# A hybrid SSD decoder block on one core: the order of SSD products and late conditioning on TensorE

## Chip, core and metric

The kernel runs on one core of a Trainium2 chip. The metric is the device time of one execution in microseconds (us); the kernel before takes 1359.24 us, the median of three runs (1358.83 to 1359.36).

## What is computed

One layer of a decoder with 2048 channels. A prompt of 256 tokens and eight samples of four tokens are processed together, so that each activation is a matrix of 2048 channels by 288 columns. In the reference, cut to what matters here:

```python
mod = silu(c) @ w_ada + b_ada                    # six parts: sh1, sc1, g1, sh2, sc2, g2
h = rmsnorm(x, norm1) * (1 + sc1) + sh1
u_pool, z, xbc, dt_raw = split(h @ w_in)
pool_out = pool_mixer(u_pool)                    # trailing means, a small product per group
y = ssd(xs * dt, dt * A, Bm, Cm, h0)             # 24 heads of 64 in 4 groups, chunks of 128
#   y_diag = (C B^T * exp(cs_l - cs_s), masked) @ xdt ; y_off = C @ h_start * exp(cs)
y = rmsnorm((y + d_skip * xs) * silu(z), ssd_norm)
x = x + g1 * (concat(pool_out, y) @ w_out)
h2 = rmsnorm(x, norm2) * (1 + sc2) + sh2
x = x + g2 * (silu(conv(h2 @ w_gate)) * (h2 @ w_val)) @ w_down
```

All is in fp32.

## The kernel before

**Weights.** A weight tile of up to 128x1024 is loaded by SyncE's queue (`load`, L259 to L263), rounded by ScalarE to a high part whi (a cast, L281), and VectorE subtracts it from the raw tile to get the low part wlo (L283). The activations have such parts too. A block of 128x128 weights then takes three products of 288 columns (`mm3`, L293 to L297): whi with the high activations, whi with the low ones, wlo with the high ones. They are called weight products below. In the stage of the change eight raw tiles and two whi and two wlo tiles are there; a new load goes out when a raw tile is free again.

**Order.** A scheduler places the instructions of every engine when the program is built, from the order in which the code emits them, their dependencies and priorities; each engine then works through its own list in order. Instructions in `tc.high_priority()` go as early as they can; `tc.keep_in_program_order` fixes an instruction behind the ones emitted before it on its engine. The emission order is set by generators that the main loops advance: `pull(generator, rate)` adds the rate to a credit and advances the generator once for each whole credit.

**Stages.** To about 186 us: the first two conditioning parts and the first blocks of the input projection. Then dt, the last block of the xbc columns and, pulled in between, the four SSD groups; then the remaining u and z columns (uz, the loop around L1030) with SSD groups still going; at about 380 us the output projection (mm_out); from 507 us the MLP (up, gate, val, down) to the end.

**An SSD group** (`ssd_group`, L710) transposes its inputs (xt, bt), forms cb = C B^T with the causal mask, the chunk states s1 and s2, and the samples' part yo: 8 products that use a quarter of the array's columns each (L771, 16 records in the trace). Then for t = 0, 1, 2, two heads at a time:
- `decays(t)` (L782): a product cse broadcasts the cumulative sums of a head; ScalarE forms relu(cs_l - cs_s) into e for three column ranges (L794) and ec by exp (L795), then exp of all of e (L796); VectorE multiplies e by cb (L797) and ec by C (L798). e and ec have two buffers each.
- `outputs(t)` (L801): ten products into one PSUM tile y, two heads side by side, 64 rows each: yo with a selection matrix (L807), xdt of the samples with e (L810), xdt of chunk 0 (L813), xdt of chunk 1 (L816), and s1 with ec (L817). VectorE adds the skip term (L819), multiplies by the gate (L823), ScalarE squares (L825) and GpSimd sums (L829).

After the groups the sum of squares goes over partitions on TensorE (ysum, L235), the reciprocal root comes back as a broadcast (pbrstdy, L248), VectorE scales the gated y (zy, L898), and ScalarE and VectorE split it into mixh (L1059) and mixl (L1060), the operands of mm_out.

**Later conditioning.** Parts 2 to 5 of mod are formed by `ada_part_units` (L397). One k step takes two raw tiles of 512 KB, each for two products of 512 columns, with sc_c (silu of the nine conditions) as a stationary operand of 32 columns at one of four column positions (`ada_mm`, L321, product L324). `AY = 2` k steps make a visit: four loads and eight products (16 records, named adap). Eight visits, a copy to SBUF (asb), four transposes (adat) and VectorE's additions (L412) finish a part. The generator `adas` (parts 2, 3, 4) is pulled in the last xbc block at RA1/AY = 0.25 for each unit, in the uz loop at RA2/AY = 0.2 for each step of two k, at TA/AY = 2 ahead of mm_out (L1038) and in mm_out's loop (L1121); part 5 has its own generator (L1126). The scheduler may put other work between a visit's products.

Of the kernel before, what the change touches and what calls it, by code (L numbers as in the profile page):

```python
# [24 lines left out]
N = NP + NS  # L25
# [25 lines left out]
GB = 4  # L51
AY = 2

RA1, RA2, RB1, RB2, RB3 = 0.5, 0.4, 1.0, 1.0, 1.0
TA, ADA_OUT = 4, 4
TK = 4
GA = (2, 3)
# [104 lines left out]
def kernel(ctx: ExitStack, tc, ins, outs):  # L162
    nc = tc.nc
# [26 lines left out]
    seli = vec[:, K_SEL:K_SEL + 32]  # L190
# [9 lines left out]
    sc_c = kp.tile([P, KT, 32], F32, name="sc_c")  # L200
# [58 lines left out]
    def load(key):  # L259
        off, cols = S.items[key]  # L260
        t = wp[0].tile([P, RAWC], F32, tag="raw", name="raw_" + "_".join(map(str, key)))
        nc.sync.dma_start(t[:, :cols], wflat[off:off + P * cols].rearrange("(p n) -> p n", p=P))
        return t  # L263
# [54 lines left out]
        return ps  # L318


    def ada_mm(ps, raw, k, c0, nb, js):  # L321
        for j in js:
            c = c0 + (j - js[0]) * nb
            nc.tensor.matmul(ps[32 * j:32 * j + 32, :nb], sc_c[:, k, :], raw[:, c:c + nb],  # L324
                             start=(k == 0), stop=(k == KT - 1), tile_position=(0, 32 * j))

    def ada_sb(ps, nb, name, r=P):
        asb = kp.tile([P, 512], F32, tag="asb", name="asb_" + name)
        nc.scalar.copy(asb[0:r, :nb], ps[0:r, :nb])
        return asb  # L330

    def ada_tr(asb, nb, name, r=P):
        pt = aux("adat_" + name)
        for i in range(nb // P):
            nc.tensor.transpose(pt[:, i * r:(i + 1) * r], asb[0:r, i * P:(i + 1) * P], ident[0:r, 0:r])
        return pt

    def ada_scale(which, part, norm, k0, gk):
        nc.vector.scalar_tensor_tensor(
            out=amul[:, which, k0:k0 + gk, :], in0=ada[:, part, k0:k0 + gk, :], scalar=1.0,  # L340
            in1=norm[:, k0:k0 + gk].unsqueeze(2).to_broadcast([P, gk, NC9]),
            op0=ALU.add, op1=ALU.mult)

    def ada_group_units(gi):
# [49 lines left out]
            nc.vector.tensor_tensor(o, src, b.unsqueeze(3).to_broadcast([P, 2, nj // 2, NC9]), ALU.add)  # L394
        ada_scale(0, 1, early[:, V_N1:V_N1 + KT], k0, gk)

    def ada_part_units(part, ay=1):  # L397
        ps = pa.tile([P, 512], F32, tag="ada", name=f"adap{part}")
        for k in range(KT):
            raws = [load(("adap", part, k, h)) for h in range(2)]  # L400
            for h in range(2):
                ada_mm(ps, raws[h], k, 0, 512, range(2 * h, 2 * h + 2))
            if k % ay == ay - 1:
                yield
        asb = ada_sb(ps, 512, f"p{part}")
        yield
        pt = ada_tr(asb, 512, f"p{part}")
        for i in range(4):
            o = ada[:, part].rearrange("p (j i) c -> p j i c", j=4)[:, :, i, :]
            b = bada[:, part].rearrange("p (j i) -> p j i", j=4)[:, :, i]  # L410
            src = pt[:, i * P:(i + 1) * P].rearrange("p (j c) -> p j c", j=4)[:, :, 0:NC9]
            nc.vector.tensor_tensor(o, src, b.unsqueeze(2).to_broadcast([P, 4, NC9]), ALU.add)  # L412
        if part == 4:
            ada_scale(1, 4, vec[:, V_N2:V_N2 + KT], 0, KT)
        yield
# [65 lines left out]
    for q in range(4):  # L481
        t = mx.tile([P, 4, N], F32, tag="blk", name=f"xa{q}", bufs=4)
# [12 lines left out]
    sx = [None]  # L495
# [205 lines left out]
    def h0b(g, b):  # L701
        return h0t[g, b // 3][:, b % 3, :]
# [4 lines left out]
    def heads(ap):  # L707
        return ap.rearrange("p (h q) -> p h q", h=HG)

    def ssd_group(g):  # L710
        cf = cfs[g]
        cff = cf.rearrange("p m n -> p (m n)")
# [8 lines left out]
        xdt = kp.tile([P, 3, G6], F32, tag="hmod", name=f"xdt{g}", bufs=2)  # L721
# [27 lines left out]
        s1 = sx[0].tile([P, G6], F32, tag="s1", name=f"s1_{g}")  # L749
# [18 lines left out]
        for i in range(2):  # L768
            for j in range(4):
                b = 4 * i + j  # L770
                nc.tensor.matmul(py[32 * j:32 * j + 32, :G6], cm[:, 32 * b:32 * b + 32],  # L771
                                 h0b(g, b), start=(i == 0), stop=(i == 1),
                                 tile_position=(0, 32 * j))
        yo = sx[0].tile([P, G6], F32, tag="yo", name=f"yo{g}")
        nc.vector.tensor_tensor(yo.rearrange("p (h q) -> p h q", h=HG),
                                py[:, :G6].rearrange("p (h q) -> p h q", h=HG),
# [4 lines left out]

        def decays(t):  # L782

            e = sx[0].tile([P, 2, N], F32, tag="e", name=f"e{g}_{t}", bufs=2)
            ec = sx[0].tile([P, 2, P], F32, tag="ec", name=f"ec{g}_{t}", bufs=2)
            for i in range(2):
                hh = HG * g + 2 * t + i
                pe = aux(f"cse{hh}")
                nc.tensor.matmul(pe[:, :N], selr[:, hh:hh + 1].to_broadcast([P, P]), csr, start=True, stop=True)


                for c in range(3):
                    n = slice(c * P, min(c * P + P, N))
                    nc.scalar.activation(e[:, i, n], pe[:, n], AF.Relu, bias=cs[:, c, hh:hh + 1], scale=-1.0)  # L794
                nc.scalar.activation(ec[:, i, :], pe[:, P:NP], AF.Exp)  # L795
            nc.scalar.activation(e, e, AF.Exp, scale=-1.0)  # L796
            nc.vector.tensor_tensor(e, e, cb.unsqueeze(1).to_broadcast([P, 2, N]), ALU.mult)  # L797
            nc.vector.tensor_tensor(ec, ec, cf[:, 4, P:NP].unsqueeze(1).to_broadcast([P, 2, P]), ALU.mult)  # L798
            return e, ec

        def outputs(t, e, ec):  # L801
            assert (g, t) in zdone
            pq = aux(f"y{g}_{t}")
            rows = [slice(0, 64), slice(64, P)]
            for i, r in enumerate(rows):
                f = slice(64 * (2 * t + i), 64 * (2 * t + i) + 64)
                nc.tensor.matmul(pq[r, NP:N], yo[:, f], seli, start=True, stop=False)  # L807
            for i, r in enumerate(rows):
                f = slice(64 * (2 * t + i), 64 * (2 * t + i) + 64)
                nc.tensor.matmul(pq[r, NP:N], xdt[:, 2, f], e[:, i, NP:N], start=False, stop=True)  # L810
            for i, r in enumerate(rows):
                f = slice(64 * (2 * t + i), 64 * (2 * t + i) + 64)
                nc.tensor.matmul(pq[r, 0:P], xdt[:, 0, f], e[:, i, 0:P], start=True, stop=True)  # L813
            for i, r in enumerate(rows):
                f = slice(64 * (2 * t + i), 64 * (2 * t + i) + 64)
                nc.tensor.matmul(pq[r, P:NP], xdt[:, 1, f], e[:, i, P:NP], start=True, stop=False)  # L816
                nc.tensor.matmul(pq[r, P:NP], s1[:, f], ec[:, i, :], start=False, stop=True)  # L817
# [5 lines left out]
            nc.vector.tensor_tensor(zt, zt, yt, ALU.mult)  # L823
            sq = kp.tile([P, N], F32, tag="xsq", name=f"ysq{g}_{t}", bufs=2)
            nc.scalar.activation(sq, zt, AF.Square)  # L825
# [81 lines left out]
    adas = chain(*(ada_part_units(p, AY) for p in (2, 3, 4)))  # L907
    with in_order(*(e.engine for e in (nc.tensor, nc.scalar, nc.vector))):
# [3 lines left out]
        for q in range(4):  # L912
# [11 lines left out]
        first = [load(("xbc", 0, ci)) for ci in range(2)]  # L924
# [59 lines left out]
    def pull(gn, rate):  # L984

        credit[id(gn)] = credit.get(id(gn), 0.0) + rate
        while credit[id(gn)] >= 1:
            credit[id(gn)] -= 1
            next(gn, None)

    nloads[0] = len(first) + KT // 4
    for bi in range(len(BLOCKS)):
        last = bi + 1 == len(BLOCKS)
        top_up()
        if last:
# [5 lines left out]
            ps = pm.tile([P, 512], F32, tag="mm", name="mm_dt")  # L1001
# [23 lines left out]
    for m in list(range(4 + 3 * ZEARLY, 16)) + ULATE:  # L1025
        for _ in uz_units(m):
            n += 1
            for gn in late.values():
                pull(gn, 0.5)
            pull(adas, RA2 / AY)  # L1030
            pull(back, RB2 if n <= zlast else RB3)
            if n == zlast:
                drain(back)
                back = chain(ssd3, y_norm())
        if m < 4:
            late[m] = pool_units(m)
            next(late[m])
# [17 lines left out]
    for g in range(4):  # L1055
        for t in range(3):
            k = 4 + 3 * g + t
# [203 lines left out]
    rstdf, _ = rstd_of(psf, D, "rstdf", False)  # L1261
# [149 lines left out]
```

## Time and profile before

| quantity | before |
|---|---|
| median of three runs | 1359.24 us |
| the profiled execution's own time | 1359.61 us |
| its span in the trace | 1357.8 us |
| TensorE (PE) busy | 1342.5 us, 99% |
| VectorE (DVE) busy | 810.1 us, 60% |
| ScalarE (ACT) busy | 578.6 us, 43% |
| GpSimd (POOL) busy | 221.0 us, 16% |
| mean granted TensorE clock | 0.997 |
| DMA, mean over the span | 238 GB/s |

The page gives the busy time of each engine, its share in 40 slices of the span, and the chain of waits that ended last. In a timeline a row is: start, duration, engine, line, operation, output<-inputs, shape, number of records, and in brackets the idle time before it with the releaser. PE's records overlap, so that the time a product costs is the distance from its start to the next one's.

### The profile page before, as it was taken

What the parts mean: (1) busy time and instruction counts of PE and PEld (TensorE: products, weight loads), DVE (VectorE), ACT (ScalarE), POOL (GpSimd) and SP (SyncE); (2) the same over time, 40 slices, a digit from 0 to 9 for tenths busy, and PEclk for the clock granted to TensorE, in tenths of its full rate; (3) what the DMA queues carried; (4) which work ended last, traced back from release to release, by engine and by line L of the source; (5) the groups of instructions that cost most, each with busy time, mean ns of one, the idle gap of its engine ahead of it and who ended that gap; (6) DMA issues with size and microseconds to landing.
All of it is one profiled execution on the core that took longest, in us unless ns stands there. A gap on an engine that the chain in (4) does not pass through costs nothing.

```text
span 1357.8 us, 26226 instructions
## 1 busy us (share of the span) xinstructions
PE 1342.5 (99%) x10557; PEld 1247.4 (92%) x10557; DVE 810.1 (60%) x1349; ACT 578.6 (43%) x908; POOL 221.0 (16%) x428
## 2 busy tenths in 40 slices
PE   9999999999999999999999999999999999999997
PEld 7889988776779889999999999999999999999996
DVE  5775568778564448645565455656654556566543
ACT  5243234587643335534443334443433344434442
POOL 0000002122221213111221001212220011222221
PEclk9999999999999999999999999999999999999998
DMA  9999668877888877777555455555554555555531
GB/s 378 405 408 355 252 216 323 335 263 288 326 302 334 310 265 257 248 293 265 184 182 184 167 176 185 197 193 182 189 178 167 183 191 185 192 200 194 180 117 71
DMA packets 97338, 323.20 MB, mean 238 GB/s; under 512 B 10752, under 2 KB 19904, under 8 KB 97216
## 3 DMA queue, kind: packets, MB, share of 16 engines
q1 hardware_dynamic: 93312, 310.64, 62.8%
q0 software_dynamic: 3184, 9.69, 1.9%
q8 instruction: 83, 1.36, 0.4%
q10 hardware_dynamic: 720, 1.19, 0.2%
q14 instruction: 39, 0.32, 0.1%
HBM read 309.78 MB, written 10.39 MB: 236 GB/s over the span
## 4 chain that ended last, share of the span: by engine, by line
PE 96%; DVE 2%; DMA 1%; ACT 0%; issue 0%; SPq 0%; POOL 0%; DVEq 0%; POOLq 0%; ACTq 0%
PE mm_down L296 7%; PE mm_down L295 7%; PE mm_down L297 7%; PE mm_val L296 6%; PE mm_gate L296 6%; PE mm_gate L295 6%; PE mm_gate L297 6%; PE mm_val L297 6%; PE mm_val L295 6%; PE xbc L295 5%; PE adap L324 5%; PE xbc L296 4%; PE xbc L297 4%; PE mm_out L295 3%; PE mm_out L296 3%; PE mm_out L297 2%
## 5 line engine op out<-in xcount | busy, mean ns | idle before, releaser
L296 PE MATMUL mm_down<-al,whi_down 128*128 128x288 f32 x688 | 202.9, 295 | 0.0
L295 PE MATMUL mm_down<-ah,whi_down 128*128 128x288 f32 x688 | 202.7, 295 | 0.0
L297 PE MATMUL mm_down<-ah,wlo_down 128*128 128x288 f32 x688 | 202.4, 294 | 0.0
L296 PE MATMUL mm_gate<-h2l,whi_gate 128*128 128x288 f32 x640 | 189.1, 296 | 0.0
L296 PE MATMUL mm_val<-h2l,whi_val 128*128 128x288 f32 x640 | 189.1, 295 | 0.0
L297 PE MATMUL mm_val<-h2h,wlo_val 128*128 128x288 f32 x640 | 188.8, 295 | 0.0
L297 PE MATMUL mm_gate<-h2h,wlo_gate 128*128 128x288 f32 x640 | 188.8, 295 | 0.0
L295 PE MATMUL mm_gate<-h2h,whi_gate 128*128 128x288 f32 x640 | 188.7, 295 | 0.0
L295 PE MATMUL mm_val<-h2h,whi_val 128*128 128x288 f32 x640 | 187.9, 294 | 0.0
L283 DVE TENSOR_TENSOR wlo_gate<-raw_gate,whi_gate 128x1024 fp32r<-128x1024 f32 x80 | 97.8, 1225 | 135.4 <-ACT whi_gate L281 135.2
L283 DVE TENSOR_TENSOR wlo_down<-raw_down,whi_down 128x1024 fp32r<-128x1024 f32 x96 | 107.5, 1119 | 116.1 <-ACT whi_down L281 115.0
L281 ACT CAST whi_down<-raw_down 128x1024 fp32r<-128x1024 f32 x96 | 92.4, 962 | 167.3 <-PE mm_down L296 118.0
L281 ACT CAST whi_gate<-raw_gate 128x1024 fp32r<-128x1024 f32 x80 | 83.9, 1051 | 159.5 <-PE mm_gate L296 67.7
L281 ACT CAST whi_val<-raw_val 128x1024 fp32r<-128x1024 f32 x80 | 84.1, 1051 | 126.0 <-issue 103.1
L295 PE MATMUL xbc<-h1h,whi_xbc 128*128 128x288 f32 x448 | 133.0, 301 | 1.2 <-ACT h1h L445 1.2
L296 PE MATMUL xbc<-h1l,whi_xbc 128*128 128x288 f32 x448 | 132.1, 296 | 0.0
L297 PE MATMUL xbc<-h1h,wlo_xbc 128*128 128x288 f32 x448 | 130.8, 297 | 0.0
L295 PEld LDWEIGHTS mm_down<-ah,whi_down 128*128 128x128 f32 x688 | 129.3, 188 | 0.0
L296 PEld LDWEIGHTS mm_down<-al,whi_down 128*128 128x128 f32 x688 | 129.3, 188 | 0.0
L297 PEld LDWEIGHTS mm_down<-ah,wlo_down 128*128 128x128 f32 x688 | 129.1, 188 | 0.0
L295 PEld LDWEIGHTS mm_gate<-h2h,whi_gate 128*128 128x128 f32 x640 | 120.5, 188 | 5.0 <-ACT ah L1176 3.4
L295 PEld LDWEIGHTS mm_val<-h2h,whi_val 128*128 128x128 f32 x640 | 120.5, 188 | 0.0
(323 smaller groups left out, 2979.3 us busy)
## 6 DMA issues: line engine op xcount, KB each, us to landing
raw_adap<-wflat SPq DMA_DIRECT2D x128, 512.0 KB, 5.5
raw_gate<-wflat SPq DMA_DIRECT2D x80, 512.0 KB, 3.5
raw_val<-wflat SPq DMA_DIRECT2D x80, 512.0 KB, 3.6
raw_ada<-wflat SPq DMA_DIRECT2D x64, 512.0 KB, 9.7
raw_xbc<-wflat SPq DMA_DIRECT2D x51, 512.0 KB, 8.9
raw_down<-wflat SPq DMA_DIRECT2D x48, 512.0 KB, 3.5
raw_out<-wflat SPq DMA_DIRECT2D x32, 512.0 KB, 6.6
raw_down<-wflat SPq DMA_DIRECT2D x32, 384.0 KB, 3.0
```

The source lines that it names most:

```text
L281: yield nc.scalar.copy(hi[:, :n], raw[:, a:a + n])
L283: yield hi, lo, nc.vector.tensor_tensor(lo[:, :n], raw[:, a:a + n], hi[:, :n].bitcast(F32), ALU.subtract)
L295: nc.tensor.matmul(ps, whi[:, w], bh, start=first, stop=False)
L296: nc.tensor.matmul(ps, whi[:, w], bl, start=False, stop=False)
L297: nc.tensor.matmul(ps, wlo[:, w], bh, start=False, stop=last)
L324: nc.tensor.matmul(ps[32 * j:32 * j + 32, :nb], sc_c[:, k, :], raw[:, c:c + nb], start=(k == 0), stop=(k == KT - 1), tile_position=(0, 32 ...
```

## The change

1. The ten products of `outputs(t)` are emitted in another order (s1 with ec first, then xdt of chunk 1, of chunk 0, of the samples, and yo with the selection matrix last), and the second to tenth are tied to the first with high priority and program order, so that nothing stands between them.
2. A visit loads its four tiles, then runs its eight products from the last tile loaded to the first, tied in the same way; `ada_mm` is gone. The new function `more()` advances `adas` by one unit with `attach` set, which ties the first product of the visit too, right behind what was emitted before it: behind the yo products, and behind `outputs(0)` and `outputs(2)` in every group. The pull in the uz loop (RA2) is gone; those in the last xbc block, ahead of mm_out and in its loop stay.
3. e and ec have three buffers each, and the product of ec is kept in program order on VectorE, behind that of e.

```diff
+    attach = [False]
+
     def ada_part_units(part, ay=1):
         ps = pa.tile([P, 512], F32, tag="ada", name=f"adap{part}")
-        for k in range(KT):
-            raws = [load(("adap", part, k, h)) for h in range(2)]
-            for h in range(2):
-                ada_mm(ps, raws[h], k, 0, 512, range(2 * h, 2 * h + 2))
-            if k % ay == ay - 1:
-                yield
+        for ka in range(0, KT, ay):
+            raws = [(k, h, load(("adap", part, k, h))) for k in range(ka, ka + ay) for h in range(2)]
+
+            tied = attach[0]
+            for k, h, raw in raws[::-1]:
+                for j in (2 * h, 2 * h + 1):
+                    with tc.high_priority() if tied else nullcontext():
+                        i = nc.tensor.matmul(ps[32 * j:32 * j + 32, :512], sc_c[:, k, :],
+                                             raw[:, (j % 2) * 512:(j % 2) * 512 + 512],
+                                             start=(k == ay - 1), stop=(k == KT - ay), tile_position=(0, 32 * j))
+                    if tied:
+                        tc.keep_in_program_order(i)
+                    tied = True
+            yield
...
+    def more():
+
+        attach[0] = True
+        next(adas, None)
+        attach[0] = False
...
                                  tile_position=(0, 32 * j))
+        more()
         yo = sx[0].tile([P, G6], F32, tag="yo", name=f"yo{g}")
...
-            e = sx[0].tile([P, 2, N], F32, tag="e", name=f"e{g}_{t}", bufs=2)
-            ec = sx[0].tile([P, 2, P], F32, tag="ec", name=f"ec{g}_{t}", bufs=2)
+            e = sx[0].tile([P, 2, N], F32, tag="e", name=f"e{g}_{t}", bufs=3)
+            ec = sx[0].tile([P, 2, P], F32, tag="ec", name=f"ec{g}_{t}", bufs=3)
...
-            nc.vector.tensor_tensor(ec, ec, cf[:, 4, P:NP].unsqueeze(1).to_broadcast([P, 2, P]), ALU.mult)
+            tc.keep_in_program_order(nc.vector.tensor_tensor(
+                ec, ec, cf[:, 4, P:NP].unsqueeze(1).to_broadcast([P, 2, P]), ALU.mult))
...
+            fs = [slice(64 * (2 * t + i), 64 * (2 * t + i) + 64) for i in range(2)]
+
+            prods = [(P, NP, lambda i: (s1[:, fs[i]], ec[:, i, :]), True, False),
+                     (P, NP, lambda i: (xdt[:, 1, fs[i]], e[:, i, P:NP]), False, True),
+                     (0, P, lambda i: (xdt[:, 0, fs[i]], e[:, i, 0:P]), True, True),
+                     (NP, N, lambda i: (xdt[:, 2, fs[i]], e[:, i, NP:N]), True, False),
+                     (NP, N, lambda i: (yo[:, fs[i]], seli), False, True)]
+            tied = False
+            for n0, n1, ops, first, last in prods:
+                for i, r in enumerate(rows):
+                    with tc.high_priority() if tied else nullcontext():
+                        ins = nc.tensor.matmul(pq[r, n0:n1], *ops(i), start=first, stop=last)
+                    if tied:
+                        tc.keep_in_program_order(ins)
+                    tied = True
+            if t != 1:
+                more()
...
-            pull(adas, RA2 / AY)
```

More of the change, by code (lines that the diff above doesn't have):

```diff
@@ L52 @@
 AY = 2
-RA1, RA2, RB1, RB2, RB3 = 0.5, 0.4, 1.0, 1.0, 1.0
+RA1, RB1, RB2, RB3 = 0.5, 1.0, 1.0, 1.0
 TA, ADA_OUT = 4, 4
@@ L318, in project @@
         return ps
[L321 to L325, printed above, removed]
     def ada_sb(ps, nb, name, r=P):
@@ L804, in outputs @@
             rows = [slice(0, 64), slice(64, P)]
[L805 to L817, printed above, removed]
+            fs = [slice(64 * (2 * t + i), 64 * (2 * t + i) + 64) for i in range(2)]
[14 more added lines that the diff above has]
+                more()
             yt = cf[:, t, 0:N]
```

## Prediction

> **What bounds the kernel now.** I read the page first (busy shares, slices, chain), then the waits of PE, then the timeline of PE, ACT and DVE in the stage that the change touches.
>
> ```profile
> span 1357.8 us, 26226 instructions
> PE 1342.5 (99%) x10557; PEld 1247.4 (92%) x10557; DVE 810.1 (60%) x1349; ACT 578.6 (43%) x908; POOL 221.0 (16%) x428
> ...
> PEclk9999999999999999999999999999999999999998
> ...
> PE 96%; DVE 2%; DMA 1%; ACT 0%; issue 0%; SPq 0%; POOL 0%; DVEq 0%; POOLq 0%; ACTq 0%
> ```
> ```profile
> PE pool L877 <- DVE pout L872: 0.7, 1, 0.7
> ...
> PE cse L789 <- DVE ada L412: 0.5, 1, 0.5
> ```
>
> PE is busy 99%, at full clock, and is 96% of the chain; its largest named waits in the changed stage are 0.7 and 0.5 us. So PE's order of work is the time: a microsecond taken out of PE there is won, unless PE then arrives before its operands. Instruction counts are the same in both kernels on every engine. PE's order is the same up to 192.55 us and, but for the order inside a visit, after 507.08 us. The sum is made for these 314.5 us of the profiled execution (1359.61 us: span 1357.8 and 1.81 around it; the median of the three runs is 1359.24, 0.37 less).
>
> **What goes from PE.** The timeline of PE, once whole and once cut up:
>
> ```profile
> 258.72 0.30 PE L296 MATMUL xbc<-h1l,whi_xbc 128*128 128x288 f32 x1
> 258.85 0.29 PE L297 MATMUL xbc<-h1h,wlo_xbc 128*128 128x288 f32 x1
> 259.07 1.92 PE L324 MATMUL adap<-raw_adap,sc_c 128*32 128x512 f32 x16
> 260.93 0.40 PE L295 MATMUL mm_uz<-h1h,whi_uz 128*128 128x288 f32 x1
> 261.16 0.29 PE L296 MATMUL mm_uz<-h1l,whi_uz 128*128 128x288 f32 x1
> ...
> 261.82 0.42 PE L789 MATMUL cse<-csr,selr 128*128 128x288 f32 x2
> ...
> 264.33 0.29 PE L295 MATMUL mm_uz<-h1h,whi_uz 128*128 128x288 f32 x1
> 264.58 0.31 PE L807 MATMUL y<-vec,yo 128*64 128x32 f32 x4
> 264.82 0.40 PE L296 MATMUL mm_uz<-h1l,whi_uz 128*128 128x288 f32 x1
> ...
> 266.08 1.91 PE L324 MATMUL adap<-raw_adap,sc_c 128*32 128x512 f32 x10
> 267.92 0.31 PE L810 MATMUL y<-e,xdt 128*64 128x32 f32 x4
> ...
> 268.89 1.06 PE L324 MATMUL adap<-raw_adap,sc_c 128*32 128x512 f32 x6
> 269.88 0.53 PE L789 MATMUL cse<-csr,selr 128*128 128x288 f32 x2
> ```
> ```profile
> 353.26 0.31 PE L807 MATMUL y<-vec,yo 128*64 128x32 f32 x4
> ...
> 354.35 0.40 PE L295 MATMUL mm_uz<-h1h,whi_uz 128*128 128x288 f32 x1
> ```
> ```profile
> L324 PE MATMUL adap<-raw_adap,sc_c 128*32 128x512 f32 x424 | 59.4, 599 | 0.0
> ```
>
> Starts are what counts, since records overlap.
> - A whole visit (16 records) takes 259.07 to 260.93, 1.86 us. The cut one takes 1.84 for its 10 records (to 267.92) and 0.99 for its 6 (268.89 to 269.88): 2.83. Each cut costs 0.97 us. The 424 records of the row stand in 35 runs in before, in 27 in the changed order: 8 cuts go, **-7.8 us**.
> - Weight products (the 128x288 ones) follow each other by 0.133 us (258.72 to 258.85). At the border to a visit or a y it is 0.22 (258.85 to 259.07; 260.93 to 261.16: 0.23), so a run of them pays about 0.1 on each side. Before has 80 such runs between other work, the changed order 54. Of these 26 some lose two such sides, some one (beside a full-width product), and next to cse nothing: 26 x about 0.165, **-4.3 us**.
> - A y in one run takes 353.26 to 354.35, 1.09 us. Scattered, it takes 0.24 (264.58 to 264.82) and 0.97 (267.92 to 268.89), 1.21. Twelve y's, some cut twice: **-1.0 us**. Fewer lone cse products: **-0.3**.
>
> Together -13.4 us on a PE that never waits. The Trainium skill, TensorEngine Tiling (Array Packing), Key Properties, says that a change of tiling mode drains the engine; that is the border cost above, and it has no rule for a visit cut in the middle, which costs ten times as much here.
>
> **Old stalls that end.** Comparing gaps with the clean ones, the window holds 3.75 us of stalls: the waits above, and records stretched by a late load or operand (in the boundary rows below, the visit's 10 records take 2.60 us instead of 1.84). All their places are reordered, so I take out **-3.75** and count the new ones in full.
>
> **What comes in: PE arrives early at the decays.** y now begins with s1 times ec, and all ten products wait until e and ec are both through ACT and DVE. In before, part of the y went ahead and weight products or visits filled the rest. One such chain in before, ACT's timeline and the DVE groups:
>
> ```profile
> 262.15 0.80 ACT L794 ACTIVATE e<-cse,csd 128x128 f32<-128x128 f32 x3 [0.62 <-PE cse L789]
> 262.96 1.28 ACT L795 ACT_TABLE_LOAD   x1
> ...
> 264.43 0.80 ACT L794 ACTIVATE e<-cse,csd 128x128 f32<-128x128 f32 x3
> ...
> 265.25 0.71 ACT L796 ACTIVATE e<-e 128x576 f32<-128x576 f32 x1
> ```
> ```profile
> L283 DVE TENSOR_TENSOR wlo_uz<-raw_uz,whi_uz 128x1024 fp32r<-128x1024 f32 x16 | 19.6, 1222 | 7.4 <-ACT whi_uz L281 5.5 <-PE mm_uz L297 1.9
> L281 ACT CAST whi_uz<-raw_uz 128x1024 fp32r<-128x1024 f32 x16 | 16.7, 1045 | 1.4 <-PE mm_uz L296 1.4
> L797 DVE TENSOR_TENSOR e<-e,cb 128x576 f32<-128x576 f32 x12 | 9.0, 753 | 0.4
> L682 ACT ACTIVATE cf<-cf 128x1280 f32<-128x1280 f32 x4 | 5.1, 1276 | 2.0 <-DVE cf L672 1.9
> L825 ACT ACTIVATE ysq<-zy 128x288 f32<-128x288 f32 x12 | 5.4, 447 | 9.1 <-DVE zy L823 9.1
> ```
>
> From the first relu (262.15, 0.33 after its cse) to the end of exp at 265.96 are 3.8 us, with e's product on DVE 4.6, one table load and no cast in it; a head without table load takes 0.82 (264.43 to 265.25). ACT's order in the changed build puts a whi_uz cast (1.05) into the middle of nearly every such chain, since raw_uz loads now stand behind a visit's four loads on the eight raw slots, and its order alternates exp with silu: 16 table loads in the SSD zone instead of 14 (1.28 each).
> - **y(t=0), groups 0 to 2.** Chain from the first cse: 0.33 + 4.6 + 1.05, 6.0 (group 0: the weight products behind the cast also wait for its subtraction, 1.22). PE's work from that cse to the y: group 1 two cse pairs, 31 weight products, 5.0; group 2 the same with 30, 5.0; group 0 four cse, a visit and 18 weight products, some 5.1. I take 2.45, 1.5 and 1.4 us of waiting, the chain's excess and, in group 1 and 2, half a microsecond for DVE's queue; 5.35 in sum.
> - **y(t=2), groups 1 and 2.** ACT between the exp of t=0 and of t=2, group 1: two heads of t=1 with exp 2 x 0.82 + 0.71 = 2.35; table load 1.28, silu of cf 1.28, ysq 0.45; then t=2 with table load and cast 3.8 + 1.05; 10.2. PE there: y 1.1, visit 1.9, cse 0.35, y 1.1, 26 weight products 3.6: 8.0. Less a lead of 0.6 that e had at y(t=0): 1.6. Group 2 has one short activation more (0.45, as ysq) and 22 products (7.5 against 10.65): 2.55. Sum 4.15.
> - Group 3, and t=2 of group 0 (51 weight products ahead): nothing; cover is longer than the chain.
>
> The third e/ec buffer lets relu of t=2 start before y(t=0) has read its e; it bounds no wait counted here, since ACT's own order does: 0. The ec product behind e on DVE instead of ahead: its 0.52 comes after e, so ec, which y now reads first, is last by about 0.5; taken as hidden by the lead, else +0.5 at each of the five stops, 2.5 in the range.
>
> **The boundary to the output projection.** DVE and PE of before:
>
> ```profile
> 371.15 0.75 PE L248 MATMUL pbrstdy<-early,r3rstdy 128*128 128x128 f32 x6
> ...
> 375.63 1.91 PE L324 MATMUL adap<-raw_adap,sc_c 128*32 128x512 f32 x10
> 378.23 0.75 PE L877 MATMUL pool<-pout,poolw 128*128 128x288 f32 x2 [0.70 <-DVE pout L872]
> ...
> 380.34 0.40 PE L295 MATMUL mm_out<-mixh,whi_out 128*128 128x288 f32 x1
> ```
> ```profile
> 372.37 1.05 DVE L898 TENSOR_TENSOR zy<-zy,pbrstdy 128x864 f32<-128x864 f32 x1 [0.72 <-ACT rstdy L253]
> 373.34 3.02 DVE L898 TENSOR_TENSOR zy<-zy,rstdy 128x864 f32<-128x864 f32 x2
> ...
> 376.72 0.53 DVE L1060 SCALAR_TENSOR_TENSOR mixl<-zy,vec,mixh 128x288 fp32r<-128x288 f32 x1
> ...
> 384.31 3.09 DVE L1060 SCALAR_TENSOR_TENSOR mixl<-zy,vec,mixh 128x288 fp32r<-128x288 f32 x7
> ```
>
> In before PE has 28 weight products and a cut visit between pbrstdy and mm_out: 9.2 us (371.15 to 380.34), and another cut visit in mm_out's first tile. The changed order leaves 3 weight products, one visit, a pool product and the transposes: 0.6 for pbrstdy, 0.5, 1.86 and 0.8, 3.8 us. DVE from pbrstdy's start in its new order: 1.22 wait, zy 1.05, zy 1.51, a wlo_out 1.22, zy 1.51, small pool and ada pieces 2.0, then the first mixl, ready at about 8.9. PE waits some 5 us for it. Then mixl come every 0.44 (3.09/7) against 0.40 for three products, the last four behind a wlo_out: the tile ends at about +17.8 where unhindered PE would end at +10.6. **+7.2 us**. The ysum ahead of it keeps 22 weight products (2.9 us) behind the last y, where before has a visit and some (1.86 and more): taken at nothing.
>
> **Sum.** New stalls 5.35 + 4.15 + 7.2 = 16.7. The moved visits also bunch 2 MB of loads ahead of each of three stops in a group:
>
> ```profile
> 192.55:380.30 187.75, 186.02 (x1458) 137.84 (x1456) 143.96 (x297) 119.83 (x241) 41.29 (x68) 1.00 0.80 295
> ```
>
> The queues carry 295 GB/s at a share of 0.80 there now; SP issues the same loads in another order, so a visit can wait for its fourth load (it runs in reverse, so none of it starts without the last). Nothing in before shows it: 0 to 2 us by the stretched visit above (0.76 each, two or three such); I take 1. So 1359.61 - 13.4 - 3.75 + 16.7 + 1.0 = 1360.2 profiled, **1359.8** as a median: the saving is given back to the decays and the boundary.
>
> **Rivals.**
> 1. *The saving stays* (faster). If the casts finish early enough that the decay chains fit under PE's work, the 9.5 us at the y's are gone: 1359.8 - 9.5 = 1350.3; with the boundary without its 7.2 as well, 1343. For it: the waits of PE in before name no e and no ec at all. Against it: those y's were scattered over more cover, and ACT's order above is fixed.
> 2. *Weights come late to every group* (slower). Place: the eight raw slots. A visit holds four of them until its last product; a raw_uz behind it is issued only then. If that load lands after PE has used up the previous half tile, PE waits for cast and subtraction (1.05 + 1.22 = 2.3) at such a stop. It decides from the point at which a load takes longer than the 2 to 4 us of products left; three such stops beyond my sum give +6.8: 1366.6.
> 3. *The wait of 5 us at the boundary lowers the clock* (slower). The clock row shows no granted clock under 0.8 anywhere, but PE never idles that long in it. If the 46 products left of the first tile ran at half clock, three products would take 0.8 against mixl's 0.44, 16 x 0.8 = 12.8 instead of 9: +3.8, 1363.6. The Trainium skill, TensorE: Matmul & The Clock Gate, HAM oscillation, states that idle gaps over about 3.4 us do halve the clock for as long again; no run here shows it, and an estimate by that page is 1.7 us.
> 4. *The change doesn't do what it says*: the runs are not unbroken. The built order has all twelve y's and all visits whole, so this only leaves "same for another reason".
>
> **How the numbers follow.** Forecast 1359.8 with its own range 1356 to 1364 (0.47); rival 1 0.30; rival 2 0.13; rival 3 0.07; rival 4 0.03. 0.2% is 2.7 us, about what a measurement of this kernel can tell from no change: bounds 1356.5 and 1362.0. The forecast's 0.47 splits into 0.02 faster, 0.28 same and 0.17 slower; rival 4 is same. So faster 0.32, same 0.31, slower 0.37. The range reaches into rivals 1 and 2: 1349 to 1367.
>
> **What would show it.** In the changed profile: visits of 16 records at 1.86 and y's of 20 at 1.09 (the first terms); waits of PE on the e or ec product, at y(t=0) of groups 0 to 2 and y(t=2) of groups 1 and 2, near 1.4 to 2.8 each; one wait of about 5 us of mm_out on mixl; table loads 1.28 between exp and silu. Wrong, if PE's waits on e and mixl sum to under 8 us (then rival 1), if visits wait for DMA by more than 2 us in all (rival 2), or if the granted clock dips behind the boundary (rival 3).

## The result and the profile after

The changed kernel takes 1372.48 us (median of five runs, 1370.04 to 1373.55) against 1359.36 us: a ratio of 1.0094, interval 1.0080 to 1.0108. It is 13 us slower, outside the predicted range of 1349 to 1367. The profiled execution took 1371.11 us with a span of 1369.3 us. Its page, the lines that answer to those of before:

```profile
span 1369.3 us, 26203 instructions
PE 1335.4 (98%) x10557; PEld 1249.4 (91%) x10557; DVE 814.8 (60%) x1349; ACT 581.2 (42%) x910; POOL 221.2 (16%) x428
PE   8999999988989999999999999999999999999997
...
PE 92%; DVE 3%; DMA 2%; ACT 2%; issue 0%; SPq 0%; POOL 0%; DVEq 0%; ACTq 0%; POOLq 0%
```

PE is busy 7.1 us less than before (1335.4 against 1342.5), so the work did shrink; it waits more. The chain lost 4 points of PE to DVE, DMA and ACT. A slice is 34.2 us long; the ones that fell below 9 are, but for the first, those from 274 to 342 us and from 377 to 411: the SSD stage and its end. PE's waits in the changed kernel (in total, times, longest):

```profile
PE mm_uz L295 <- ACT whi_uz L281: 7.6, 5, 2.6
PE mm_out L296 <- DVE mixl L1075: 4.8, 1, 4.8
PE mm_uz L297 <- DVE wlo_uz L283: 3.8, 5, 0.8
PE mm_up L295 <- ACT h2h L449: 2.6, 1, 2.6
...
PE y L828 <- DVE ec L809: 0.9, 2, 0.5
```

The y's hardly wait for their decays (0.9 us). PE stops a few products ahead of them, at a weight product whose whi or wlo isn't there: 11.4 us in five places. Two of the five, with the clean parts around them, in PE's timeline:

```profile
288.32 1.90 PE L402 MATMUL adap<-raw_adap,sc_c 128*32 128x512 f32 x16
290.15 0.53 PE L800 MATMUL cse<-csr,selr 128*128 128x288 f32 x2
...
296.23 0.40 PE L295 MATMUL mm_uz<-h1h,whi_uz 128*128 128x288 f32 x1 [2.50 <-ACT whi_uz L281]
296.47 0.29 PE L296 MATMUL mm_uz<-h1l,whi_uz 128*128 128x288 f32 x1
297.49 0.40 PE L297 MATMUL mm_uz<-h1h,wlo_uz 128*128 128x288 f32 x1 [0.73 <-DVE wlo_uz L283]
...
303.67 0.44 PE L828 MATMUL y<-ec,s 128*64 128x128 f32 x4
303.94 0.69 PE L828 MATMUL y<-e,xdt 128*64 128x128 f32 x12
304.47 0.29 PE L828 MATMUL y<-vec,yo 128*64 128x32 f32 x4
304.68 0.40 PE L296 MATMUL mm_uz<-h1l,whi_uz 128*128 128x288 f32 x1
```

A whole visit takes 1.83 us (288.32 to 290.15) and an unbroken y 1.01 us (303.67 to 304.68), where the prediction had 1.86 and 1.09. The loss is in the waits between them. Why whi_uz was late shows in ACT's and in SP's queue for the same stretch, first ACT:

```profile
290.59 0.80 ACT L805 ACTIVATE e<-cse,csd 128x128 f32<-128x128 f32 x3 [2.55 <-PE cse L800]
291.40 1.28 ACT L806 ACT_TABLE_LOAD   x1
292.69 0.28 ACT L806 ACTIVATE ec<-cse 128x128 f32<-128x128 f32 x1
292.87 0.36 ACT L805 ACTIVATE e<-cse,csd 128x128 f32<-128x128 f32 x1
295.13 1.04 ACT L281 CAST whi_uz<-raw_uz 128x1024 fp32r<-128x1024 f32 x1 [1.90 <-DMA raw_uz<-wflat]
```
```profile
283.30 4.99 SPq L702 DMA_DIRECT2D h<-h  x2
289.41 0.34 SPq L262 DMA_DIRECT2D raw_uz<-wflat  x1
289.80 7.99 SPq L262 DMA_DIRECT2D raw_adap<-wflat  x4
```

The raw_uz load goes out at 289.41, in the middle of the visit that started at 288.32, lands at 295.11, 5.7 us later, and its cast starts at 295.13. ACT stands for 1.90 us in front of that cast, with the rest of the first decays behind it in the same queue. So one late weight tile delays both the products and the y. What SP itself had waited for, from 280 to 290 us and, ahead of the other stop of 2.6 us, from 328.5 to 333:

```profile
SPq L262 <- DVE ada L416: 5.0, 1, 5.0
SPq L702 <- PE yo L781: 4.1, 1, 4.1
SPq L262 <- PE adap L402: 1.1, 1, 1.1
```
```profile
SPq L262 <- PE adap L402: 2.8, 2, 2.3
SPq L262 <- PE cse L800: 0.4, 1, 0.4
```

Before the first stop SP's queue stood for 5.0 us at the fourth load of a visit, which went out at 282.92. (The view puts that wait down to ada; VectorE's subtraction that reads a raw_uz tile, 1.22 us from 281.67, ended at 282.89 too.) Behind it came the loads of h, which waited for yo's products, and then the weight load itself waited for a raw tile that the visit had to give back. Before the second stop it was nearly all such tiles. A visit runs from its last tile to its first, so the first of its four to be loaded comes free last. The last thing to see is the granted clock, in stretches of 1 us (length, busy time of PE, PEld, DVE, ACT and POOL, then clock, DMA share and GB/s):

```profile
298.00:299.00 1.00, 1.00 (x9) 0.83 (x9) 0.94 (x3) 1.00 (x7) 0.00 (x0) 0.88 0.48 176
299.00:300.00 1.00, 1.00 (x12) 1.00 (x12) 0.00 (x0) 0.98 (x3) 0.00 (x0) 0.50 0.83 325
...
301.00:302.00 1.00, 1.00 (x8) 0.20 (x4) 1.00 (x3) 1.00 (x1) 0.00 (x0) 0.50 0.30 104
302.00:303.00 1.00, 1.00 (x12) 0.12 (x4) 0.61 (x2) 0.55 (x2) 0.00 (x0) 0.91 0.00 0
...
389.00:390.00 1.00, 0.00 (x0) 0.00 (x0) 1.00 (x6) 1.00 (x4) 0.00 (x0) 0.50 0.93 315
...
393.00:394.00 1.00, 1.00 (x6) 1.00 (x5) 1.00 (x3) 0.28 (x1) 0.00 (x0) 0.50 1.03 420
394.00:395.00 1.00, 1.00 (x9) 1.00 (x8) 1.00 (x4) 0.00 (x0) 0.60 (x3) 0.83 0.55 221
```

PE is busy from 298 to 303 us and has half its clock for most of it: 0.12 + 3 x 0.50 + 0.09 = 1.7 us lost. A second such dip follows the wait of 2.6 us at 338 us, and a third, 2.1 us in PE's busy time, goes with the wait for mixl at the output projection.

What the clock takes differs between executions of the same kernel: the five runs have a mean granted clock of 0.993 (1370.04 and 1371.11 us), 0.992 (1372.48) and 0.989 (1373.03 and 1373.55). The profile is of one that lost little.

### The profile page after: what moved, and what is told of

Its sections match the earlier page's. It is cut to its first block, busy times and chain, and to the rows that moved or that the text cites. A ratio compares the mean times of both kernels' runs of the same rounds, so it can differ in the third digit from the quotient of the medians.

```text
span 1369.3 us, 26203 instructions
## 1 busy us (share of the span) xinstructions
PE 1335.4 (98%) x10557; PEld 1249.4 (91%) x10557; DVE 814.8 (60%) x1349; ACT 581.2 (42%) x910; POOL 221.2 (16%) x428
## 3 DMA queue, kind: packets, MB, share of 16 engines
q10 hardware_dynamic: 720, 1.19, 0.2%
## 4 chain that ended last, share of the span: by engine, by line
PE 92%; DVE 3%; DMA 2%; ACT 2%; issue 0%; SPq 0%; POOL 0%; DVEq 0%; ACTq 0%; POOLq 0%
PE mm_down L296 7%; PE mm_down L295 7%; PE mm_down L297 7%; PE mm_val L296 6%; PE mm_gate L296 6%; PE mm_gate L295 6%; PE mm_val L297 6%; PE mm_gate L297 6%; PE mm_val L295 6%; PE xbc L295 4%; PE xbc L297 4%; PE xbc L296 4%; PE adap L402 3%; PE mm_out L295 3%; PE mm_out L296 3%; PE mm_out L297 3%
## 5 line engine op out<-in xcount | busy, mean ns | idle before, releaser
L281 ACT CAST whi_val<-raw_val 128x1024 fp32r<-128x1024 f32 x80 | 84.1, 1051 | 129.1 <-issue 111.6
L296 PEld LDWEIGHTS mm_down<-al,whi_down 128*128 128x128 f32 x688 | 129.1, 188 | 0.0
```

The source lines that it names most:

```text
L281: yield nc.scalar.copy(hi[:, :n], raw[:, a:a + n])
L296: nc.tensor.matmul(ps, whi[:, w], bl, start=False, stop=False)
```

## The experiments

Two theories were set against each other. **Theory A**, the slots: a visit's four loads stand ahead of the weight loads in the eight raw tiles, so weights, and the decay chain behind their casts, come late; clock and boundary add to it. **Theory B**, the prediction's own: y waits as one block for e and ec, whose chain on ACT has lost its cover. Each ratio below is to the kernel before, with its interval.

### One part at a time

The first run ties the y products only:

```diff
-                nc.tensor.matmul(pq[r, NP:N], yo[:, f], seli, start=True, stop=False)
...
+            for n0, n1, ops, first, last in prods:
+                for i, r in enumerate(rows):
+                    with tc.high_priority() if tied else nullcontext():
+                        ins = nc.tensor.matmul(pq[r, n0:n1], *ops(i), start=first, stop=last)
+                    if tied:
+                        tc.keep_in_program_order(ins)
```

> Only the y products are tied into one run in the new order (visits, decays and their buffers as before). Theory A (the visits' four loads ahead of the weight loads are what delays PE): PE keeps its visits as cover and the weight loads their slots, so no wait on whi_uz over 1 us; time 1357 to 1360. Theory B (the decay chain is uncovered because y waits as one block for e and ec): waits of 1.4 to 2.5 us at five y's, time 1364 to 1368.

Measured: 1362.71 us, 1.0026 (1.0016 to 1.0035). Slower by 3 us, between the two expectations, and for neither's reason: PE waits 2.4 us for mixl and 1.2 for ysum's operand, 0.4 for ec, and nothing over 0.2 for weights; behind the wait for mixl the clock is at half from 385.6 to 389.0 us, which costs 1.7. Eight of the twelve y's also stayed in two pieces (the fixed order on DVE, ec behind e, is missing here; whether that is why wasn't tried), and the visits stand in 36 runs instead of 35. So it says little on unbroken y's.

The second run makes the visits whole, without moving them:

```diff
-            for h in range(2):
-                ada_mm(ps, raws[h], k, 0, 512, range(2 * h, 2 * h + 2))
+        for ka in range(0, KT, ay):
+            raws = [(k, h, load(("adap", part, k, h))) for k in range(ka, ka + ay) for h in range(2)]
+            for k, h, raw in raws[::-1]:
...
             pull(adas, RA2 / AY)
```

> Only the visits run whole, in reverse order of their loads, pulled at the places and rates of before; y as before. Theory A: eight cuts of 0.97 us go, and no visit stands right ahead of a cse, so weight loads are late at most once: 1350 to 1355. Theory B: the cuts go and the y's are scattered as before: 1350 to 1353. If whole visits as such cost the time (their last load waited for): 1360 or more.

Measured: 1359.07 us, 0.9997 (0.9987 to 1.0006): no change, and both theories had expected a gain of 4 us or more. From start to start the 424 records of the visits take about 8.4 us less than in before. Most of it is given back in waits: 2.0 us for pout and 1.9 for mixl around the first products of the output projection, 0.8 for dtt and 1.3 for h2h, where before waits 0.7 for pout, 0.4 for mixl and for neither of the others. And the clock dips behind the wait for mixl, which costs another 1.7 us of busy PE:

```profile
380.00:381.00 1.00, 1.00 (x5) 1.00 (x6) 1.00 (x4) 0.00 (x0) 0.00 (x0) 0.50 1.01 399
...
382.00:383.00 1.00, 1.00 (x6) 1.00 (x5) 0.87 (x3) 0.33 (x1) 0.00 (x0) 0.50 1.05 426
383.00:384.00 1.00, 1.00 (x9) 0.71 (x11) 1.00 (x4) 0.11 (x1) 0.00 (x0) 0.81 1.02 418
```

The third adds the attachment:

```diff
+        more()
         yo = sx[0].tile([P, G6], F32, tag="yo", name=f"yo{g}")
...
+            if t in (0, 2):
+                more()
...
-            pull(adas, RA2 / AY)
```

> Whole visits tied behind the yo products and behind y of t=0 and t=2, pull in the uz loop gone; y scattered as before, decays with two buffers. Theory A: nearly the whole loss is here: casts that wait for raw_uz and PE that waits for whi_uz at 2 to 2.6 us twice, 4 to 5 us of wait for mixl at the boundary, clock under 0.8 behind each: 1368 to 1373. Theory B: the scattered y's do not wait as a block; only the boundary's wait of 5 us stays: 1357 to 1361.

Measured: 1370.75 us, 1.0079 (1.0064 to 1.0094). With y still scattered and two buffers it stands 11.2 us above before, of the change's 13. Its waits:

```profile
PE mm_uz L295 <- ACT whi_uz L281: 5.7, 4, 2.5
PE mm_out L296 <- DVE mixl L1078: 4.8, 1, 4.8
PE mm_up L295 <- ACT h2h L455: 1.7, 1, 1.7
```

They are the changed kernel's in kind (wlo_uz has only 0.5 us here), so placing the visits behind yo and y, and not the y's, makes the weights late: A against B. The third buffer was undone by itself:

```diff
-            e = sx[0].tile([P, 2, N], F32, tag="e", name=f"e{g}_{t}", bufs=3)
-            ec = sx[0].tile([P, 2, P], F32, tag="ec", name=f"ec{g}_{t}", bufs=3)
+            e = sx[0].tile([P, 2, N], F32, tag="e", name=f"e{g}_{t}", bufs=2)
+            ec = sx[0].tile([P, 2, P], F32, tag="ec", name=f"ec{g}_{t}", bufs=2)
```

> The changed kernel with two buffers each for e and ec again; its order on TensorE is the same product for product. If the third buffers matter, PE waits more at y of t=2 and the time rises by 1 us or more over the changed kernel's 1372.5; if ScalarE's own order bounds the decays, as the prediction said, 1371 to 1374.

Measured: 1375.54 us (1371.15 to 1376.73), 1.0112 (1.0095 to 1.0129). The interval overlaps the changed kernel's; the waits in its trace are the same (7.1 for whi_uz, 4.8 for mixl). Whether the third buffer is worth something up to 3 us stays unclear, the more so as the granted clock differs between the four runs (0.991 at 1371.15 us, 0.987 and 0.988 at the others); it isn't what makes the kernel slow.

### Slots and loads

One raw tile more, paid for with the third e and ec buffers, so that the last run is its comparison:

```diff
+            wx[0] = mx_ctx.enter_context(tc.tile_pool(name="wx", bufs=1, reuse_waits="tile"))
+            wp[0].add(wx[0], 1, 0)
```

> As the run with two buffers, and the memory saved is one raw weight tile more, nine instead of eight, in the SSD stage. Slot theory (a visit's four loads hold slots, so the next raw_uz is issued late and its cast, with the decay chain behind it, too): the casts' waits for the DMA of raw_uz (1.9 and 0.9 us) go, PE's waits for whi_uz halve from 7.6 us: 1366 to 1369. Theory that ScalarE's order alone (cast behind relu and table load) makes PE wait: 1371 to 1374.

Measured: 1365.01 us, 1.0045 (1.0030 to 1.0060): 10.5 us faster than its comparison and 7.5 faster than the changed kernel, more than expected, from one tile of memory. Waits for whi_uz fall from 7.1 to 3.9 us, those for wlo_uz from 3.4 to 2.0. The order on PE changes a little with it, so not all of it need be the slot.

With the eight tiles of the changed kernel, but each raw_uz load issued half a tile earlier:

```diff
+    def ahead_uz():
+        if nextuz:
+            k2 = nextuz.popleft()
+            rawuz[k2] = load(k2)
...
+            hi, lo = ready.pop(key + (h,), None) or split(rawuz.pop(key + (h,), None) or load(key + (h,)), 0, n * P,
+                                                          f"{name}_{h}")
+            if key[0] == "uz":
+                ahead_uz()
```

> The changed kernel with each raw_uz load issued one half tile earlier, ahead of the visit that stood before it; slots as before. Slot theory: raw_uz lands in time, but a visit's last load is pushed back instead: waits for whi_uz below 3 us in sum, some waits of adap for its loads: 1366 to 1370. Theory of ScalarE's order: 1371 to 1374 with waits for whi_uz as before (7 us).

Measured: 1361.80 us, 1.0016 (1.0006 to 1.0025): 10.7 us of the 13 are back, again more than expected, with nothing edited but when weights are fetched (the scheduler then places some weight products otherwise, too). Its waits:

```profile
PE mm_out L296 <- DVE mixl L1088: 4.9, 1, 4.9
PE y L839 <- DVE ec L820: 2.2, 2, 1.4
PE mm_uz L295 <- ACT whi_uz L281: 2.0, 2, 1.7
```

Waits for whi_uz are 2.0 instead of 7.6 us and those for wlo_uz 0.7 instead of 3.8, and with them the two dips are gone: the clock is 1.00 from 290 to 310 and from 335 to 345 us. Only now does theory B's wait appear, with 2.2 us at y. The wait for mixl is untouched.

Is the early load worth something by itself? The same edit on the kernel before:

> The kernel before with nothing but the raw_uz loads one half tile earlier. Slot theory, taken strictly: in the kernel before no cast waits long for raw_uz, so nothing to win, 1358 to 1360. If early uz weights are worth something by themselves (then the gain of the run with loads ahead says little on the change): 1352 or less.

Measured: 1365.27 us, 1.0044 (1.0029 to 1.0059): 6 us slower, which neither case had expected. The scheduler then cuts the visits in four more places (39 runs of records instead of 35, 3.7 us from start to start), PE waits 2.7 us for mixl, and the clock is at half twice, from 373.4 to 376.8 and from 387.1 to 390.5 us. So early loads showed no gain in themselves; in the changed kernel they undo a harm.

### The clock

A filler of 34 products that nobody reads (FILL) was to take the place of the wait for mixl:

```diff
+                    nc.tensor.matmul(ps[:, :N], hi[:, 0:P], bh, start=True, stop=False)
+                    fl = aux("fill")
+                    for _ in range(FILL):
+                        with tc.high_priority():
+                            tc.keep_in_program_order(
+                                nc.tensor.matmul(fl[:, :N], hi[:, 0:P], bh, start=True, stop=True))
```

> The changed kernel with 34 products of the same size more, into a PSUM tile that nobody reads, between the first and second product of the output projection, where PE waited 4.75 us for mixl. If that wait lowered the clock behind it (0.59, 0.50 and 0.78 in three stretches of 3 us), the added work makes the kernel faster: about 2 us less than the changed one, 1370, and the granted clock stays 1.00 from 387 to 396 us. If the clock has another cause: the same time, 1372 to 1373, with the same clock.

Measured: 1378.38 us, 1.0131 (1.0111 to 1.0152). It missed: the pool product behind it was scheduled ahead of the filler and waited 5.4 us for pout, so that the idle time stayed and the 34 products came on top. It tells nothing on the clock. The filler was moved ahead of that, with FILL = 16:

```diff
     pull(adas, TA / AY)
+    fl = aux("fill")
+    for _ in range(FILL):
+        with tc.high_priority():
+            tc.keep_in_program_order(
+                nc.tensor.matmul(fl[:, :N], ones, early[:, 0:N], start=True, stop=True))
```

> The changed kernel with 16 full-fp32 products of 288 columns (about 0.28 us each, 4.4 us) into an unread PSUM tile, this time right behind the last visit ahead of the output projection, so that they stand in the wait for mixl. Clock theory: the wait is gone, the granted clock stays 1.00 behind it, and the kernel with more work is about 2 us faster: 1370 to 1371. Without a clock effect: 1372 to 1374.

Measured: 1373.45 us, 1.0102 (1.0084 to 1.0119), the changed kernel's time. But its 16 products took 7.9 us instead of 4.4, 0.49 each. The stretch from the start of pbrstdy to the last product of mm_out is 129.1 us, against 128.5 in the changed kernel: 7.9 us of useless work cost 0.7, and the clock stayed at 1.00 in this stretch. With nine instead of 16:

> As the second filler, which took 7.9 us because each of its products took 0.49 and not 0.28 us, now with 9 of them, 4.4 us, the length of the wait. The stretch from the start of pbrstdy to the 96th product of the output projection was 24.4 us in the changed kernel (381.03 to 405.44), 25.1 with 7.9 us of filler. Clock theory: 22 to 23 us and the granted clock stays at 1.00. Without a clock effect: 24.4 or more. In the whole time at most 2 us, near what its runs scatter: 1369 to 1373.

Measured: 1370.40 us (1368.40 to 1376.60), 1.0089 (1.0065 to 1.0113); in whole time that isn't told from the changed kernel. The place itself is clear, in PE's timeline and in stretches of 3 us:

```profile
390.75 4.63 PE L1059 MATMUL fill<-early,ones 128*128 128x288 f32 x18
395.01 0.51 PE L296 MATMUL mm_out<-mixh,whi_out 128*128 128x288 f32 x1
```
```profile
390.00:393.00 3.00, 3.00 (x17) 1.82 (x10) 3.00 (x3) 2.46 (x6) 2.70 (x4) 1.00 0.62 205
393.00:396.00 3.00, 2.51 (x11) 1.71 (x9) 3.00 (x13) 2.38 (x6) 0.55 (x1) 1.00 1.03 356
```

The clock stays at 1.00, and pbrstdy to the last product of mm_out takes 127.1 us: 1.4 less than in the changed kernel, with 4.3 us more work in it. (The 96th product can't be compared, since a visit moved in front of it.) So the half clock there comes from the idle PE. In the SSD stage, which the fillers don't touch, the profiles of these two runs have four and five dips and lose 8.0 and 11.3 us to them, where the changed kernel's has two and loses 3.4; they are of executions of 1375.47 and 1376.60 us, the longest of their runs. So their whole times say little. These two fillers multiply fp32 ones, not rounded weights.

### The gain, without the attachment

Whole visits and early loads, y as before:

> Whole visits that aren't tied behind anything, pulled as in the kernel before, y scattered, raw_uz one half tile earlier. The eight cuts are gone; whole visits alone gave 1359.1, waits at the boundary (mixl, pout, adat: about 6 us) having taken the gain. Slot theory: few waits for whi_uz were left there, so 1356 to 1359; what the boundary takes stays.

Measured: 1359.86 us, 1.0003 (0.9994 to 1.0013). PE waits for no weights; the gain goes in 5.0 us of waiting for mixl and a dip of the clock with it (378.0 to 384.8 us, 2.0 us of busy PE). And with unbroken y's, three buffers and the changed order on DVE:

> Unbroken y's, whole visits pulled as in the kernel before and tied behind nothing, three buffers and the changed order on VectorE, raw_uz one half tile earlier: the change without its attachment. PE has 24 to 39 weight products ahead of most y's. Slot theory: waits for whi_uz and e under 3 us, the clean 13 us won, less about 7 for the boundary: 1352 to 1356. If unbroken y's cost a wait in any place: 1360 or more.

Measured: 1356.58 us, 0.9978 (0.9968 to 0.9987): this version beats both kernels. All twelve y's are whole, from start to start 12.1 us against 14.7 in before, and the visits take 8.4 us less. Its waits:

```profile
PE mm_out L296 <- DVE mixl L1086: 5.0, 1, 5.0
PE y L838 <- DVE ec L819: 1.7, 3, 0.7
PE mm_up L295 <- ACT h2h L466: 1.4, 2, 0.8
```

pbrstdy starts at 366.9 us instead of 371.2, 4.3 us earlier with ten instead of 28 uz products left behind it. What remains of the saving stands in front of mixl, and in a dip from 377.2 to 380.6 us, 1.7 us, that follows. Three more runs asked whether visits held back for that place would cover the wait (the edit is against the run before):

```diff
-RA1, RA2, RB1, RB2, RB3 = 0.5, 0.4, 1.0, 1.0, 1.0
-TA, ADA_OUT = 4, 4
+RA1, RA2, RB1, RB2, RB3 = 0.5, 0.25, 1.0, 1.0, 1.0
+TA, ADA_OUT = 8, 4
```

With these, three visits stand behind pbrstdy; with RA2 = 0.2 and TA = 12, in the second and third run, four.

> As the run with unbroken y's, untied whole visits and early loads (1356.6 us), but the visits come at 0.125 for each step of the uz loop instead of 0.2, and four units are pulled ahead of the output projection instead of two: three visits stand between pbrstdy and its first product. Cover theory: the wait for mixl falls from 5.0 to about 2 us, the clock stays at 1.00: 1352 to 1354. Chain theory (VectorE ends later by as much): 1356 or more. If the visits now missing in the SSD groups uncover the decays there: waits at y.

Measured: 1356.59 us, 0.9977 (0.9967 to 0.9987): the same time, so the cover theory's time missed, although its mechanism came: the wait for mixl is gone, and in its place PE waits 3.0 us for pout and 2.5 for the loads of the visits themselves, and the clock dips there too (368.2 to 371.6 us).

> The same with 0.1 for each step and six units: four visits, 7.4 us, between pbrstdy and the first product. Cover theory: no wait for mixl at all, 1350 to 1353, if the SSD groups stay covered. Chain theory: 1356 or more.

Measured: 1362.39 us, 1.0021 (1.0012 to 1.0031): 5.8 us slower than with three. pbrstdy starts at 360.3 us, but then:

```profile
PE adap L419 <- DMA raw_adap<-wflat: 8.1, 3, 4.1
```

Four visits in a row need 16 loads in one place, and the visits wait for them. So cover there is bounded by the same loads that hurt in the SSD groups.

> As the last one, but raw_uz is loaded as in the kernel before and the changed one, not earlier. Fewer visits stand in the SSD groups, so slots are free and the early loads should matter little: within 2 us of the last one, if the slot theory holds; 4 us or more behind it if the early loads act on their own.

Measured: 1363.77 us, 1.0029 (1.0017 to 1.0041), 1.4 us behind the last: where few visits stand in the SSD groups, early loads hardly matter, as the slot theory has it.

## Why the prediction was wrong

**The clean saving** was right or too small. The visits' records run at 1.83 us whole, and unbroken y's at 1.01 us; the run without attachment has 8.4 and 2.6 us less on the two (7.8 and 1.0 predicted; the prediction's own 0.12 for each of twelve y's would have made 1.4). PE's busy time fell by 7.1 us although the half clock stretched it by 5.5. The 4.3 us for borders weren't measured alone.

**The waits at the y's** were put at 9.5 us, with e and ec as their reason. They are 7.6 + 3.8 + 0.9 = 12.3 us, nearly all ahead of the five y's named, but 11.4 of it is for whi_uz and wlo_uz. The step that failed is the sentence that costs the visits' loads: "0 to 2 us by the stretched visit above (0.76 each, two or three such); I take 1". It looked for a visit waiting for its own last load, and the row that it took for one was misread: of the 2.60 us behind 375.63 in before, 1.91 are the visit's ten records and 0.70 is the pool product's wait for pout, which the prediction lists among the waits as well. No visit of before waited for a load, and none of the changed kernel did. What the runs showed is the opposite: visits get theirs, and the weight load behind them in SP's queue and in the eight tiles comes late (1.90 us of ACT's idle time at one cast). One tile more is worth 7.5 us against the changed kernel and 10.5 against its own comparison, an earlier load 10.7. That is rival 2, which had a chance of 0.13 and a time of 1366.6; it was there with its mechanism, and was thought of as coming on top of waits for e that in fact it replaces.

**The boundary** was predicted well: a wait of about 5 us for mixl (measured 4.75), and the first output tile's end at 17.8 us behind the start of pbrstdy (measured 18.0 to the 49th product). The 17.8 is in part luck: it has no half clock in it. With nine fillers and the clock at 1.00 the 48th product starts 18.5 us behind pbrstdy with a visit of 1.86 ahead of it, so 16.6 without it, against 17.8 in the changed kernel.

**The clock**, rival 3, was given 0.07 and one place, with 3.8 us. It fell in three: 1.7 us behind each of the two longest waits for weights and 2.1 behind mixl, 5.5 in all. The sum took the waits and never asked what follows a wait of that length. The row of 40 slices, from which it read that no granted clock is under 0.8, averages over 34 us: in the trace of before the clock is 0.50 from 1351 us on, 3 us behind PE's last product, where it costs nothing but shows what idle time brings. The Trainium skill, TensorE: Matmul & The Clock Gate, What's actually happening, had it: half the clock after an idle window of about 3.4 us, until PE has been busy for about as long. The length of the dips agrees: each is 3.4 us (298.8 to 302.2) or a multiple (6.8 us at mixl, 387.5 to 394.3; 10.3 with four visits held back, 366.6 to 376.9). The 1.7 us that the prediction worked out by that page is what each of the first two cost. The trigger doesn't follow from the length of one wait: 2.50 and 0.73 us with two products between brought a dip, and so did a single one of 1.19 (ahead of 373.4 us in the kernel before with early loads), while the 2.59 us for h2h brought none. At 265 us, 1.67 and 0.73 us brought none in the changed kernel's profile and a dip in those with fillers, where the two waits are the same.

**The next boundary** was taken as unchanged. From the last product of mm_out to the first of mm_up before takes 7.3 us (128.6 to 135.9 us behind pbrstdy), the changed kernel 9.3: h2h stands on ACT behind a cast of weights that waits for its load:

```profile
517.56 0.83 ACT L281 CAST whi_upk<-raw_upk 128x768 fp32r<-128x768 f32 x1 [2.62 <-DMA raw_upk<-wflat]
518.30 0.76 ACT L449 CAST h2h<-h_n 128x288 fp32r<-128x288 f32 x2
```

The visits of part 5 there are whole too. That these are what delays raw_upk wasn't tried.

So the stage of the sum, from the product at 192.57 us in before (192.97 in the changed kernel) to the first mm_up, grew by 11.3 us (314.5 to 325.8) where the sum had 0.6: 2.8 for more waits at the y's, 3.4 for the clock there, 2.0 at the next boundary. The 1.0 us for visits waiting didn't come, so that some 3.5 us are not settled; 0.7 of them is a wait for dtt. That whole visits alone gain nothing although PE works 8.4 us less is only in part traced: 2.8 us more for pout and mixl, the dip of 1.7 behind them, 0.8 for dtt and 1.3 for h2h. Which of the operations on VectorE ahead of the output projection would have to go was not tried.

## What to carry to other kernels

When a step is made unbroken, look at what its inputs hold while they wait: four loads tied to one place took half of the buffers that the weights needed, and an engine that works in order passed the delay of one cast on to everything behind it. A saving on an engine that is 99% busy shows up as a wait at the next chain that is as long as before, so ask of each stage end what is late next. And price a wait with what follows it: in these traces the matmuls ran at half clock for 3.4 us or a multiple behind waits of 1.2 to 5 us, though not behind all of them, which is 1.7 us lost for each 3.4 in which PE is busy.

## What was not expected of the hardware

- The clock halved while PE was working again: 2.7 us after the end of the 2.50 us wait (296.23 to 298.9 us), and in the wait for mixl already during it.
- A product of full fp32 with 288 columns, a constant from early as moving operand, took 0.47 to 0.49 us in the fillers, with two records each, against 0.133 us for a weight product of the same shape.
- Useless matmuls in a wait were nearly free or better: 7.9 us of them made their stretch 0.7 us longer, 4.3 us made it 1.4 us shorter. The gain is in the stretch; in whole time neither run is told from the changed kernel.
- The changed kernel's five runs spread over 3.5 us, with the lower granted clock in the longer ones; those of the kernel before spread over 0.8 us.
